# Attention scores of the window and sparse branches as full-array products, probabilities scaled on GpSimd

## The chip, the cores and the metric

The kernel runs on one core of a Trainium2 chip. TensorE (PE) does matrix products and transposes, VectorE (DVE), ScalarE (ACT) and GpSimd (POOL) do the rest, and DMA queues move data; the queue called SP here only issues DMAs. The metric is the device time of one execution in microseconds (us), the median of the runs.

## The reference, cut to what matters

A stack of layers on 512 tokens of width 1024 with 256 context tokens. Two layers of a first block hold, beside a convolution branch, a neighbourhood attention (NA) and a window attention (WA) with 8 heads of 64; later come a recurrent layer, a feed-forward layer, a sparse attention layer (NSA) with 16 heads and a second feed-forward layer. All values are float32. The parts that the change touches:

```python
# WA: block n of 128 queries sees up to 3 blocks of keys and 256 context keys
s_w = einsum('bqkgd,bskd->bkgqs', q_n, k_n) * scale
s_w = where(valid, s_w, -inf)
s_c = einsum('bqkgd,bnkd->bkgqn', q_n, k_ctx) * scale
m = maximum(max(concat([s_w, s_c]), axis=-1), sink)
e = exp(s - m)
p = e / (sum(e) + exp(sink - m))
# NSA: three branches (compressed, selected, window), each gated
s = einsum('bgrqd,bgkd->bgrqk', qc, kw)
s = s - slope * dist
p = masked_softmax(s, mask)
o = gc[0] * o_cmp + gc[1] * o_sel + gc[2] * o_win
```

## The kernel before, in words

**Number format.** Every float32 operand of a product is split into a rounded part (hi) and a rest (lo), `k.split` (L199 for the part on ACT, L200 for the rest on DVE). A product is then three: hi by hi, hi by lo, lo by hi. The large weights are loaded by SP, cast on ACT (L126, `wh`) and subtracted on DVE (L127, `wl`); their products stand at L140 to L142 (moving operand of 512 columns) and L151 to L153 (256 columns). These are called GEMM products here.

**Attention in units.** NA and WA are worked in units of one block of 128 queries (`attend`, L653). The score products of a unit (`att_qk`, `scores`, L484 to L490) write PSUM; `att_sm` makes probabilities; `att_tr` transposes them on PE (L582, L585) and copies them back; `pv` multiplies with V. In WA a pair of heads has one query block with both heads at its two ends (bands of 256 keys) and, for the two middle blocks, one unit for each head (bands of 384 keys): 16 one-head and 8 two-head units in a layer. In the first layer 8 further units come, of context queries, with 256 context keys alone. A unit is closed (transposed and multiplied) when more than three (WA) stand open.

**Half-array score products.** A head has 64 channels, and two heads lie on the two halves of the 128 partitions. The score products of before use 64 rows of the array each (form 64*128 in the trace): for one head three products, for two heads six, three in either half.

**Softmax of WA.** For each head: a maximum over the context scores (L543), a maximum with the sink (L545), an add of the mask with a running maximum over the band (L548), a negation (L551), the exponential on ACT (L553, or L556 and L557), the exponential of the sink (L561), sum and reciprocal, and the scaling of the probabilities on DVE (L570).

**NSA.** The loop L1530 to L1550 goes over 8 values of f (two heads each). In each f there are eight score units, two branches by four query blocks in the order 1, 3, 2, 0 with 256, 512, 384 and 256 columns, and one compressed unit. That makes 64 units: 32 of 256 columns, 16 of 384 and 16 of 512. L1459 has the scores, L1488 the mask and the maximum, L1490 the exponential, L1492 the scaling on DVE, L1524 the transposes, L1527 their copies. A unit is closed two units after its scores. `queries` (L1430) makes the queries of the next f as fill: 24 GEMM products, then `qf` (L1434) on DVE and the split into `nQ`.

**What sets the order.** A generator of attention steps is woven with a generator of GEMM steps: each attention step returns a cost, and GEMM steps are put behind it until the cost, times a ratio, is paid (`weave`, L55; in NSA the sum `due`, ratio 0.32). The framework's scheduler then sets the order on each engine from dependences and priorities, and puts in the waits.

Of the kernel before, what the change touches and what calls it, by code (L numbers as in the profile page):

```python
# [19 lines left out]
P = 128  # L20
# [16 lines left out]
NA_N, NW_N = (0, 0, 0, 0), (0, 0, 0, 0)  # L37
# [178 lines left out]
def first_block(k):  # L216
# [74 lines left out]
    for l in range(2):  # L291
# [120 lines left out]
        with tc.tile_pool(reuse_waits="tile", name=f"att{l}", bufs=2) as ap:  # L412
# [57 lines left out]

            def to_T_nat(raw, dst, g):
# [11 lines left out]

            def scores(heads, dst, Q, qi, K_, ki, q0, k0, kn):  # L484

                for a, b in ((0, 0), (0, 1), (1, 0)):
                    for i in heads:
                        sl = slice(64 * i, 64 * i + 64)
                        nc.tensor.matmul(dst[i], Q[sl, a, qi, q0:q0 + P], K_[sl, b, ki, k0:k0 + kn],  # L489
                                         start=a + b == 0, stop=a == 1)  # L490

            def att_qk(un):
# [35 lines left out]
                scores(heads, sc_, Q, qi, K_, ki, qb * P, 512, 256)  # L528
                if nb:
                    scores(heads, sb, Q, qi, K_, ki, qb * P, un["band"][0] * P, nb)  # L530
                return len(heads) * 3 * (256 + nb) / 2400

            nrm_ = [0]

            def att_sm(un):
# [3 lines left out]
                for i in un["heads"]:  # L539
# [3 lines left out]
                    V.tensor_reduce(m[:, 0:1], sc_, axis=AX.X, op=ALU.max)  # L543
                    if sink is not None:
                        V.tensor_max(m[:, 0:1], m[:, 0:1], sink)  # L545
                    mx = m[:, 0:1]
                    if nb:
                        V.tensor_tensor_reduce(out=sb, in0=sb, in1=un["bias"][i], scale=1.0, scalar=m[:, 0:1],  # L548
                                               op0=ALU.add, op1=ALU.max, accum_out=m[:, 1:2])
                        mx = m[:, 1:2]  # L550
                    V.tensor_scalar(m[:, 2:3], mx, -1.0, None, op0=ALU.mult)  # L551
                    if one:
                        AC.activation(pr, un["S"][i][:, :nb + 256], AF.Exp, bias=m[:, 2:3], accum_out=m[:, 3:4])  # L553
                        tot = m[:, 3:4]
                    else:
                        AC.activation(pr[:, nb:nb + 256], sc_, AF.Exp, bias=m[:, 2:3], accum_out=m[:, 3:4])  # L556
                        AC.activation(pr[:, :nb], sb, AF.Exp, bias=m[:, 2:3], accum_out=m[:, 4:5])  # L557
                        V.tensor_add(m[:, 5:6], m[:, 3:4], m[:, 4:5])
                        tot = m[:, 5:6]
                    if sink is not None:  # L560
                        AC.activation(m[:, 6:7], sink, AF.Exp, bias=m[:, 2:3])  # L561
# [4 lines left out]
                    nrm_[0] += 1  # L566
                    if (NA_N, NW_N)[not un["grp"]["na"]][nrm_[0] % 4]:
# [1146 lines left out]
```

## Time and profile before

| quantity | value |
|---|---|
| median of 3 runs | 2898.27 us (2898.22 to 2898.31) |
| profiled execution | 2899.95 us |
| its span, first to last instruction | 2898.1 us |
| mean granted TensorE clock | 0.993 of full speed |
| busy share of the span: PE, DVE, ACT, POOL | 98%, 67%, 38%, 0% |

The profile is of one execution. A row of the timeline gives the start, the duration, the engine, the line and operation, the output and inputs and their shape, and in brackets how long the engine was idle before and what released it. A row of several like instructions (x3) has the start of the first and the time until the last one's end. Ends of matrix products are modelled, so the time that a product holds PE is read from one start to the next, not from its duration. The stages of the attention branches are, in us from the span's start: NA of the first layer 117 to 254, WA 328 to 480, NA of the second layer 1000 to 1115, WA 1172 to 1275, NSA 2235 to 2440.

### The profile page before, as it was taken

What the parts mean: (1) busy time and instruction counts of PE and PEld (TensorE: products, weight loads), DVE (VectorE), ACT (ScalarE), POOL (GpSimd) and SP (SyncE); (2) the same over time, 40 slices, a digit from 0 to 9 for tenths busy, and PEclk for the clock granted to TensorE, in tenths of its full rate; (3) what the DMA queues carried; (4) which work ended last, traced back from release to release, by engine and by line L of the source; (5) the groups of instructions that cost most, each with busy time, mean ns of one, the idle gap of its engine ahead of it and who ended that gap; (6) DMA issues with size and microseconds to landing.
All of it is one profiled execution on the core that took longest, in us unless ns stands there. A gap on an engine that the chain in (4) does not pass through costs nothing.

```text
span 2898.1 us, 41445 instructions
## 1 busy us (share of the span) xinstructions
PE 2839.2 (98%) x15812; PEld 2313.7 (80%) x15812; DVE 1941.7 (67%) x4673; ACT 1114.6 (38%) x2218; POOL 0.7 (0%) x6
## 2 busy tenths in 40 slices
PE   6999999999999999999999999999999999999998
PEld 3987877888887888778888878888888666888886
DVE  5767788994544667999757866636543777663663
ACT  3444454122222444542334743223333766322221
POOL 0000000000000000000000000000000000000000
PEclk8999999999999999999999999999999999999999
DMA  6211111432125221112233233232243001223322
GB/s 219 69 62 46 36 33 42 146 131 73 66 73 161 84 74 62 44 59 91 99 106 105 95 96 100 89 107 95 88 134 103 23 16 52 95 93 97 102 89 78
DMA packets 79542, 248.68 MB, mean 86 GB/s; under 512 B 8944, under 2 KB 16496, under 8 KB 79344
## 3 DMA queue, kind: packets, MB, share of 16 engines
q1 hardware_dynamic: 75888, 238.69, 25.6%
q10 hardware_dynamic: 3456, 7.34, 0.8%
q8 instruction: 125, 2.05, 0.3%
q14 instruction: 73, 0.60, 0.1%
HBM read 239.71 MB, written 4.19 MB: 84 GB/s over the span
## 4 chain that ended last, share of the span: by engine, by line
PE 88%; DVE 5%; ACT 2%; issue 1%; DMA 0%; DVEq 0%; ACTq 0%
PE g L140 22%; PE g L142 22%; PE g L141 22%; PE g L151 3%; PE g L153 2%; PE g L152 2%; PE s L489 2%; PE g L1508 1%; PE o L609 1%; PE t L585 1%; PE t L582 1%; PE s L1459 1%; PE s L516 1%; PE t L1524 1%; PE o L630 1%
## 5 line engine op out<-in xcount | busy, mean ns | idle before, releaser
L126 ACT CAST wh<-wr 128x1024 fp32r<-128x1024 f32 (+2 forms) x392 | 392.3, 1002 | 839.0 <-PE g L141 581.8
L140 PE MATMUL g<-Hh,wh 128*128 128x512 f32 x1736 | 691.1, 398 | 0.5 <-DVE Yb L1255 0.4
L141 PE MATMUL g<-Hl,wh 128*128 128x512 f32 x1736 | 682.2, 393 | 0.0
L142 PE MATMUL g<-Hh,wl 128*128 128x512 f32 x1736 | 681.3, 392 | 0.0
L127 DVE TENSOR_TENSOR wl<-wr,wh 128x1024 fp32r<-128x1024 f32 (+2 forms) x392 | 455.2, 1162 | 304.8 <-ACT wh L126 303.9
L140 PEld LDWEIGHTS g<-Hh,wh 128*128 128x128 f32 x1736 | 326.6, 188 | 75.7 <-issue 5.9
L142 PEld LDWEIGHTS g<-Hh,wl 128*128 128x128 f32 x1736 | 326.1, 188 | 71.9 <-issue 2.3
L141 PEld LDWEIGHTS g<-Hl,wh 128*128 128x128 f32 x1736 | 326.6, 188 | 63.7 <-issue 1.0
L151 PE MATMUL g<-wh,Hh 128*128 128x256 f32 x640 | 187.6, 293 | 1.6 <-ACT Hh L359 1.3
L915 DVE SCALAR_TENSOR_TENSOR cv<-apad,cv 128x499 f32<-128x499 f32 (+23 forms) x305 | 187.1, 668 | 0.6
L153 PE MATMUL g<-wh,Hl 128*128 128x256 f32 x640 | 183.0, 287 | 0.0
L152 PE MATMUL g<-wl,Hh 128*128 128x256 f32 x640 | 182.9, 286 | 0.0
L141 PE MATMUL g<-fl,wh 128*128 128x512 f32 x384 | 149.6, 390 | 0.0
L142 PE MATMUL g<-fh,wl 128*128 128x512 f32 x384 | 149.6, 390 | 0.0
L140 PE MATMUL g<-fh,wh 128*128 128x512 f32 x384 | 149.6, 390 | 0.0
L151 PEld LDWEIGHTS g<-wh,Hh 128*128 128x128 f32 x640 | 123.1, 192 | 9.5 <-issue 5.9
L153 PEld LDWEIGHTS g<-wh,Hl 128*128 128x128 f32 x640 | 122.4, 192 | 4.5 <-issue 2.9
L152 PEld LDWEIGHTS g<-wl,Hh 128*128 128x128 f32 x640 | 123.0, 192 | 1.7 <-issue 1.2
L1276 DVE TENSOR_TENSOR fxp<-g,nb 128x512 f32<-128x512 f32 x48 | 33.2, 692 | 127.4 <-PE g L142 127.4
L553 ACT ACTIVATE pr<-s,m 128x512 f32<-128x512 f32 (+1 forms) x128 | 80.6, 633 | 76.8 <-DVE m L551 65.9
L1168 DVE TENSOR_TENSOR Xs<-Xs,g 128x512 f32<-128x512 f32 x48 | 33.0, 688 | 113.0 <-PE g L142 112.9
L140 PE MATMUL g<-Ch,wh 128*128 128x256 f32 x352 | 101.2, 287 | 0.0
(403 smaller groups left out, 5249.7 us busy)
## 6 DMA issues: line engine op xcount, KB each, us to landing
wr<-in_ffn_w_in_dram SPq DMA_DIRECT2D x96, 512.0 KB, 3.5
wr<-in_w_in_t_dram SPq DMA_DIRECT2D x88, 512.0 KB, 3.5
wada<-in_w_ada_dram SPq DMA_DIRECT2D x48, 512.0 KB, 4.6
wr<-in_ffn_w_out_dram SPq DMA_DIRECT2D x64, 384.0 KB, 3.1
wr<-in_w_in_n_dram SPq DMA_DIRECT2D x32, 512.0 KB, 3.8
wr<-in_lru_w_in_dram SPq DMA_DIRECT2D x20, 512.0 KB, 3.5
wr<-in_w_o_dram SPq DMA_DIRECT2D x16, 512.0 KB, 3.6
bt<-in_nab_dram SPq DMA_DIRECT2D x48, 128.0 KB, 2.4
```

Of the source, the lines that this page charges most:

```text
L126: nc.scalar.copy(h[:, :n], r[:, :n])
L127: nc.vector.tensor_sub(lo[:, :n], r[:, :n], h[:, :n].bitcast(F32))
L140: mm(o, a, hi(k), start=k == 0, stop=False)
L141: mm(o, a, lo(k), start=False, stop=False)
L142: mm(o, b, hi(k), start=False, stop=k == KT - 1)
L151: mm(o, h, w[k][0], start=k == 0, stop=False)
L152: mm(o, h, w[k][1], start=False, stop=False)
L153: mm(o, lo(k)[:, t0:t0 + P], w[k][0], start=False, stop=k == KT - 1)
L489: nc.tensor.matmul(dst[i], Q[sl, a, qi, q0:q0 + P], K_[sl, b, ki, k0:k0 + kn], start=a + b == 0, stop=a == 1)
L553: AC.activation(pr, un["S"][i][:, :nb + 256], AF.Exp, bias=m[:, 2:3], accum_out=m[:, 3:4])
L915: V.scalar_tensor_tensor(d, src, wc, d, op0=ALU.mult, op1=ALU.add)
L1276: V.tensor_mul(xp[:, 2:514], o, rb)
```

## The change

**Scores.** The two WA and NSA score functions now use all 128 rows. A query tile of one head holds its hi part on one half of the partitions and its lo part on the other half; the keys stand doubled on both halves. One product with the keys' hi part gives hi by hi plus lo by hi, a second with the keys' lo part gives hi by lo plus lo by lo: two products for each head where there were three. The part that lies on the wrong half is first made in a helper tile (`tmp`, `qx`) and brought over by DMA: in WA two DMAs for each transposed group, issued from POOL (`swap`), in NSA two of 64x512 (128 KB each) for each f, issued from SP. Casts and subtractions go over half the partitions, two of each instead of one. Bands of 256 and context are scored together in 512 columns.

**Softmax of WA.** One instruction over band and context adds the mask (zeros for the context), negates, and takes the running minimum from the negated sink; the maximum over the context, the one with the sink and the negation go. With a band of 384 keys there are two such instructions.

**Scaling.** All probabilities (160 instructions in NA and WA, 128 in NSA) are scaled on POOL instead of DVE.

**Costs for the order.** The score steps return two thirds of the cost they returned, so less GEMM work is put between.

```diff
             def to_T2(raw, dst, g, gain, tmp):
...
+                for lo, h, l_ in ((0, d4[0:64, :, 0, c], x[0:64]), (64, x[64:128], d4[64:128, :, 1, c])):
+                    sl = slice(lo, lo + 64)
+                    AC.activation(h, tv[sl], AF.Identity, scale=gain[sl])
+                    V.scalar_tensor_tensor(l_, tv[sl], gain[sl], h.bitcast(F32), op0=ALU.mult, op1=ALU.subtract)
+                swap(d4, x, c)
+            def swap(d4, x, c):
+                nc.gpsimd.dma_start(out=d4[64:128, :, 0, c].bitcast(F32), in_=x[0:64].bitcast(F32))
+                nc.gpsimd.dma_start(out=d4[0:64, :, 1, c].bitcast(F32), in_=x[64:128].bitcast(F32))
+            def to_T2_nat(raw, dst, g, tmp):
...
+                if g == 1:
+                    swap(dst.rearrange("p (a i) n -> p a i n", i=2), tmp, slice(0, S))
-            def scores(heads, dst, Q, qi, K_, ki, q0, k0, kn):
+            def scores(na, heads, dst, Q, qi, K_, ki, q0, k0, kn):
+                if not na:
+                    for i in heads:
+                        for b in range(2):
+                            kk = K_[:, b, ki, k0[0]:k0[0] + kn]
...
+                            nc.tensor.matmul(dst[i], Q[:, 2 * qi + i, q0:q0 + P], kk, start=b == 0, stop=b == 1)
+                    return
-                return len(heads) * 3 * (256 + nb) / 2400
+                return len(heads) * (3 if na else 2) * (256 + nb) / 2400
...
+                        both = one and nb
+                        for x, bias, to in (((un["S"][i], wmz(un["bias"][i], z), m[:, 1:2]),) if both else
+                                            ((sc_, z, m[:, 0:1]),) + (((sb, un["bias"][i], m[:, 1:2]),) if nb else ())):
...
+                            V.tensor_tensor_reduce(out=x, in0=x, in1=bias, scale=-1.0, scalar=mx,
+                                                   op0=ALU.add, op1=ALU.min, accum_out=to)
+                            mx = to
...
-                        V.tensor_scalar(pr, pr, rc, None, op0=ALU.mult)
+                    G.tensor_scalar(pr, pr, rc, None, op0=ALU.mult)
...
-                k.split(Q[:, 0], Q[:, 1], qf)
+                k.split(Q[0:64, 0], qx[0:64], qf[0:64])
+                k.split(qx[64:128], Q[64:128, 1], qf[64:128])
+                nc.sync.dma_start(out=Q[64:128, 0].bitcast(F32), in_=qx[0:64].bitcast(F32))
+                nc.sync.dma_start(out=Q[0:64, 1].bitcast(F32), in_=qx[64:128].bitcast(F32))
...
-                for x, y in ((0, 0), (0, 1), (1, 0)):
-                    for i in range(2):
-                        nc.tensor.matmul(S_[i][:, :nn], Q[sls[i], x, qb * P:(qb + 1) * P], KS[b][sls[i], y, g, :nn],
-                                         start=x + y == 0, stop=x == 1)
-                return 6 * nn / 2400
+                for i in range(2):
+                    for y in range(2):
+                        nc.tensor.matmul(S_[i][:, :nn], Q[:, i, qb * P:(qb + 1) * P], KS[b][:, y, g, :nn],
+                                         start=y == 0, stop=y == 1)
+                return 4 * nn / 2400
...
-                    V.tensor_scalar(pr[:, :nk], pr[:, :nk], m[:, 2:3], GT[:, qb, h:h + 1], op0=ALU.mult, op1=ALU.mult)
+                    G.tensor_scalar(pr[:, :nk], pr[:, :nk], m[:, 2:3], GT[:, qb, h:h + 1], op0=ALU.mult, op1=ALU.mult)
```

The order on PE in the first WA stage of the first layer, before; the names s are score tiles in PSUM, g the GEMM output, kw and qw the WA keys and queries:

```order
L152 MATMUL g_3855<-wl_3758,Hh_99 128x256
L489 MATMUL s_3931<-kw_3024,qw_3449 128x256 x3
L153 MATMUL g_3855<-wh_3757,Hl_100 128x256
L151 MATMUL g_3855<-wh_3751,Hh_99 128x256
L152 MATMUL g_3855<-wl_3752,Hh_99 128x256
L153 MATMUL g_3855<-wh_3751,Hl_100 128x256
L151 MATMUL g_3855<-wh_3751,Hh_99 128x256
L152 MATMUL g_3855<-wl_3752,Hh_99 128x256
L489 MATMUL s_3932<-kw_3024,qw_3449 128x384 x3
L153 MATMUL g_3855<-wh_3751,Hl_100 128x256
```

The same place after (the score line is now L531, the GEMM lines L150 to L152):

```order
L152 MATMUL g_3876<-wh_3767,Hl_100 128x256
L531 MATMUL s_3882<-kw_3026,qw_3451 128x512 x2
L531 MATMUL s_3911<-kw_3026,qw_3451 128x256 x2
L531 MATMUL s_3912<-kw_3026,qw_3451 128x384 x2
L150 MATMUL g_3876<-wh_3773,Hh_99 128x256
L151 MATMUL g_3876<-wl_3774,Hh_99 128x256
L531 MATMUL s_3932<-kw_3026,qw_3451 128x256 x2
L152 MATMUL g_3876<-wh_3773,Hl_100 128x256
```

Three score products of 256 or 384 columns have become two, and a two-head unit two pairs of 512 columns.

The order on PE in NSA between one f and the next, before: transposes of the old f (L1524), then the scores of the new f (L1459, nQ is its query tile), with the compressed scores (L1451) between:

```order
L1524 MATMUL t_21478<-ident,pr_21407 128x128 x4
L1524 MATMUL t_21484<-ident,pr_21407 128x128 x4
L1451 MATMUL s_21500<-KC,qf_21201 128x62 x4
L1524 MATMUL t_21516<-ident,pr_21435 128x128 x3
L1524 MATMUL t_21521<-ident,pr_21435 128x128 x3
L1459 MATMUL s_21526<-KS_20040,nQ_21492 128x256
L1459 MATMUL s_21527<-KS_20040,nQ_21492 128x256
L1459 MATMUL s_21526<-KS_20040,nQ_21492 128x256
L1459 MATMUL s_21527<-KS_20040,nQ_21492 128x256
L1459 MATMUL s_21561<-KS_20040,nQ_21492 128x512
L1459 MATMUL s_21562<-KS_20040,nQ_21492 128x512
L1459 MATMUL s_21561<-KS_20040,nQ_21492 128x512
```

The same place after (L139 to L141 GEMM, L1602 transposes, L1586 products with V, L1579 transposes of the compressed unit); g_21210 is the output from which the new f's queries are made, g_21514 that of the f after it:

```order
L141 MATMUL g_21210<-Hh_19239,wl_21207 128x512
L1602 MATMUL t_21457<-ident,pr_21388 128x128 x3
L1602 MATMUL t_21462<-ident,pr_21388 128x128 x3
L1602 MATMUL t_21502<-ident,pr_21418 128x128
L1602 MATMUL t_21505<-ident,pr_21418 128x128
L139 MATMUL g_21514<-Hh_19239,wh_21510 128x512
L140 MATMUL g_21514<-Hl_19240,wh_21510 128x512
L1586 MATMUL g_21539<-PT_21287,VS_19714 64x512
L1586 MATMUL g_21539<-PT_21288,VS_19714 64x512
L1586 MATMUL g_21539<-PT_21287,VS_19714 64x384
L141 MATMUL g_21514<-Hh_19239,wl_21511 128x512
L1579 MATMUL t_21535<-ident,pc_21446 124x128
```

The last product of the query GEMM now stands ahead of the last transposes, and GEMM products of the f after it and products with V stand where the new scores stood.

The order on ACT at the same place, before:

```order
L1490 ACTIVATE pr_21467,m_21468<-s_21459,m_21468 128x128
L199 CAST nQ_21492<-qf_21490 128x512
L1490 ACTIVATE pr_21467,m_21473<-s_21460,m_21473 128x128
L126 CAST wh_21553<-wr_21551 128x1024
L1527 COPY PT_21446<-t_21516 128x3x128
L1527 COPY PT_21447<-t_21521 128x3x128
```

and after, where L198 is the cast of the split (nQ, and qx in the helper tile), L125 the cast of the weights, L1519 the scaled bias and L1605 the copies of transposed probabilities:

```order
L198 CAST nQ_21472<-qf_21470 64x512
L125 CAST wh_21510<-wr_21508 128x1024
L198 CAST qx_21473<-qf_21470 64x512
L1519 ACTIVATE M_21480<-nb_19238 128x512 x2
L1605 COPY PT_21399<-t_21502 128x128
L1605 COPY PT_21400<-t_21505 128x128
```

The one cast of the queries is two, with the cast of the next weights between them.

## Rows read from the trace of the kernel before

**Rows 1.** page, busy time of each engine, share of the span and instructions

```profile
PE 2839.2 (98%) x15812; PEld 2313.7 (80%) x15812; DVE 1941.7 (67%) x4673; ACT 1114.6 (38%) x2218; POOL 0.7 (0%) x6
```

**Rows 2.** page, chain that ended last: share of the span by engine

```profile
PE 88%; DVE 5%; ACT 2%; issue 1%; DMA 0%; DVEq 0%; ACTq 0%
```

**Rows 3.** windows, WA stage of both layers and sparse stage: us, busy (count) by engine, clock

```profile
328.00:480.00 152.00, 149.81 (x939) 113.92 (x939) 128.98 (x527) 77.79 (x242) 0.00 (x0) 1.00 0.10 31
...
1172.00:1275.00 103.00, 102.76 (x576) 71.77 (x575) 91.72 (x359) 56.98 (x172) 0.00 (x0) 1.00 0.11 37
...
2235.00:2440.00 205.00, 200.12 (x1315) 130.63 (x1313) 156.77 (x600) 146.86 (x446) 0.00 (x0) 0.99 0.08 24
```

**Rows 4.** timeline of PE, first layer, one-head unit: start us, us, instruction

```profile
334.99 0.28 PE L151 MATMUL g<-wh,Hh 128*128 128x256 f32 x1
335.11 0.28 PE L152 MATMUL g<-wl,Hh 128*128 128x256 f32 x1
335.32 0.61 PE L489 MATMUL s<-kw,qw 64*128 64x256 f32 x3
335.86 0.39 PE L153 MATMUL g<-wh,Hl 128*128 128x256 f32 x1
...
336.77 0.78 PE L489 MATMUL s<-kw,qw 64*128 64x384 f32 x3
337.48 0.39 PE L153 MATMUL g<-wh,Hl 128*128 128x256 f32 x1
```

**Rows 5.** lines by form, PE, first WA stage: score products, busy and mean ns

```profile
L489 PE MATMUL s<-kw,qw 64*128 64x256 f32 x192 | 27.5, 307 | 0.2
...
L489 PE MATMUL s<-kw,qw 64*128 64x384 f32 x48 | 11.9, 353 | 0.0
```

**Rows 6.** timeline of PE, sparse stage, groups of 256 and 512 columns

```profile
2277.21 0.40 PE L142 MATMUL g<-Hh,wl 128*128 128x512 f32 x1
2277.53 0.62 PE L1459 MATMUL s<-KS,nQ 64*128 64x256 f32 x6
2278.09 0.88 PE L1524 MATMUL t<-ident,pr 128*128 128x128 f32 x6
2278.89 0.96 PE L1459 MATMUL s<-KS,nQ 64*128 64x512 f32 x6
2279.78 0.33 PE L1524 MATMUL t<-ident,pr 128*128 128x128 f32 x1
```

**Rows 7.** lines by form, DVE, first WA stage and sparse stage: count, busy us, mean ns

```profile
L570 DVE TENSOR_SCALAR pr<-pr,rc 128x512 f32<-128x512 f32 x16 | 7.7, 482 | 0.2
...
L1492 DVE TENSOR_SCALAR pr<-pr,m,GT 128x512 f32<-128x512 f32 x32 | 17.4, 544 | 0.4
```

**Rows 8.** lines by form, POOL, whole program

```profile
masks.py:199 POOL TENSOR_SCALAR_AFFINE_SELECT ident<-ident 128x128 f32<-128x128 f32 x1 | 0.3, 292 | 0.1
```

**Rows 9.** DMA issues: line, queue, count, KB each, median us to landing

```profile
bt<-in_nab_dram SPq DMA_DIRECT2D x48, 128.0 KB, 2.4
...
cD<-ct SPq DMA_DIRECT2D x4, 256.0 KB, 3.9
```

**Rows 10.** timeline of all engines, start of the sparse stage

```profile
2237.62 0.39 PE L142 MATMUL g<-Hh,wl 128*128 128x512 f32 x1
...
2238.78 0.62 ACT L199 CAST nQ<-qf 128x512 fp32r<-128x512 f32 x1 [5.35 <-DVE qf L1434]
...
2239.30 1.05 ACT L126 CAST wh<-wr 128x1024 fp32r<-128x1024 f32 x1
...
2239.43 0.69 DVE L200 TENSOR_TENSOR nQ<-qf,nQ 128x512 fp32r<-128x512 f32 x1 [0.68 <-ACT nQ L199]
...
2239.45 1.34 PE L1459 MATMUL s<-KS,nQ 64*128 64x256 f32 x8 [1.43 <-ACT nQ L199]
```

**Rows 11.** windows, just behind that start

```profile
2240.00:2244.00 4.00, 4.00 (x13) 2.21 (x13) 3.28 (x9) 3.58 (x8) 0.00 (x0) 0.64 0.21 56
```

**Rows 12.** waits in the sparse stage: us in total, times, longest us

```profile
PEld s L1459 <- ACT nQ L199: 5.2, 7, 1.9
```

More of the change, by code (lines that the diff above doesn't have):

```diff
@@ L527, in att_qk @@
                 un["sc"], un["sb"] = sc_, sb
-                scores(heads, sc_, Q, qi, K_, ki, qb * P, 512, 256)
-                if nb:
-                    scores(heads, sb, Q, qi, K_, ki, qb * P, un["band"][0] * P, nb)
-                return len(heads) * 3 * (256 + nb) / 2400
-            nrm_ = [0]
+                na = un["grp"]["na"]
+                if nb == 256:
+                    two = lambda v: v.rearrange("p (s n) -> p s n", s=2)
+                    scores(na, heads, {i: two(S_[i]) for i in heads}, Q, qi, K_, ki, qb * P, (un["band"][0] * P, S), 256)
+                else:
+                    scores(na, heads, sc_, Q, qi, K_, ki, qb * P, (S,), 256)
+                    if nb:
+                        scores(na, heads, sb, Q, qi, K_, ki, qb * P, (un["band"][0] * P,), nb)
+                return len(heads) * (3 if na else 2) * (256 + nb) / 2400
+            nsk = lc.tile([P, 8], F32, tag="nsk", name=k.nm("nsk"), bufs=2)
+            V.tensor_scalar(nsk, co[:, C_SINK:C_SINK + 8], -1.0, None, op0=ALU.mult)
+            zero = []
             def att_sm(un):
@@ L551, in att_sm @@
-                    V.tensor_scalar(m[:, 2:3], mx, -1.0, None, op0=ALU.mult)
+                        sg, mx = -1.0, nsk[:, un["head"][i]:un["head"][i] + 1]
+                        z = un["zero"]
+                        both = one and nb
+                        for x, bias, to in (((un["S"][i], wmz(un["bias"][i], z), m[:, 1:2]),) if both else
+                                            ((sc_, z, m[:, 0:1]),) + (((sb, un["bias"][i], m[:, 1:2]),) if nb else ())):
+                            if both:
+                                x = x.rearrange("p (s n) -> p s n", s=2)
+                            V.tensor_tensor_reduce(out=x, in0=x, in1=bias, scale=-1.0, scalar=mx,
+                                                   op0=ALU.add, op1=ALU.min, accum_out=to)
+                            mx = to
+                    else:
+                        V.tensor_reduce(m[:, 0:1], sc_, axis=AX.X, op=ALU.max)
+                        mx = m[:, 0:1]
+                        if nb:
+                            V.tensor_tensor_reduce(out=sb, in0=sb, in1=un["bias"][i], scale=1.0, scalar=mx,
+                                                   op0=ALU.add, op1=ALU.max, accum_out=m[:, 1:2])
+                            mx = m[:, 1:2]
+                        V.tensor_scalar(m[:, 2:3], mx, -1.0, None, op0=ALU.mult)
+                        mx = m[:, 2:3]
@@ L565, in att_sm, with wmz @@
                     V.reciprocal(rc, tot)
[L566 to L570 removed]
+                    G.tensor_scalar(pr, pr, rc, None, op0=ALU.mult)
+            def wmz(bias, z):
+                return bass.AP(tensor=bias.tensor, offset=bias.offset,
+                               ap=[list(bias.ap[0]), [z.offset - bias.offset, 2], [1, 256]])
             def att_tr(un):
@@ L664, in attend @@
                                           "qi": pr, "K": Kt, "ki": kis[pr],
-                                          "sink": {i: sinkf(4 * u + 2 * pr + i) for i in heads}})
+                                          "sink": {i: sinkf(4 * u + 2 * pr + i) for i in heads},
+                                          "head": {i: 4 * u + 2 * pr + i for i in heads}, "zero": natural and zero[0]})
                 def close(un):
```

61 lines of the change are left out of this document (40 added, 21 removed).

## The prediction

> **What bounds the kernel now.** I read the busy times first: TensorE (PE) is busy for 98% of the span, VectorE (DVE) for 67%, GpSimd (POOL) not at all [rows 1]. The chain that ended last says the same in another way: 88% of it is PE [rows 2]. So a saving counts only where it takes time off PE, and a wait costs as soon as PE has nothing else in its queue. Then the windows of the three stages that the change reaches: PE is busy for 149.81 of 152 us and 102.76 of 103 us in the two WA stages and 200.12 of 205 in the sparse one; DVE has 23, 11 and 48 us to spare there [rows 3]. Moving work off DVE buys nothing by itself. What is to be gained is the score products' time on PE; what can be lost is PE's full queue. The timeline of PE gives the products' real price, from start to start.
>
> **WA scores.** GEMM products of 256 columns start 0.12 us apart; when a half-array product follows, 0.21, so entering a half-array group costs 0.09. A one-head unit holds PE for 0.54 us with its three products of 256 columns and for 0.71 with its three of 384 [rows 4]. With two entries that is 1.43 us. After the change it is two products of 0.12 and two of some 0.175 (between 0.12 and the 0.23 of 512 columns, below), 0.59 us, so 0.84 less. The 48 products of 384 columns in the first stage [rows 5] are 16 such units, 32 in both layers: 27 us. Where context and band stand without GEMM between, an entry less is saved; I take 25. The other 24 units (16 with two heads, 8 of context queries; part of the 192 products of 256 columns [rows 5]) run their heads side by side, as the sparse groups below, and gain about 0.15 each, 4 us. WA: -29. If the entry is not due to the half array it stays, which leaves about 21; if leaving a group also costs something that I have not counted, it is some 6 more.
>
> **Sparse scores.** A GEMM product of 512 columns takes 0.32 with an entry behind it, so 0.23 without. A group of six products of 256 columns holds PE for 0.56 us, one of 512 for 0.89 [rows 6]; with the entry 0.65 and 0.98. Four full products are 0.48 and 0.92; for 384, between, about 0.81 and 0.70. So the 64 units save 32 x 0.17 + 16 x 0.11 + 16 x 0.06 = 8 us; groups broken into two or three parts by the scheduler pay more entries, and I take -10 (ends -4, the entry stays, and -16).
>
> The gain per unit is small where both halves were in use, since the pairs already ran side by side.
>
> **The swap in the sparse stage.** Here the change adds a wait. Today the first score needs only the cast: from the last GEMM product at 2237.62 to the score at 2239.45 it is 1.83 us, with PE idle for 1.43 [rows 10]. Afterwards a score needs lo and hi on opposite halves: after the cast (0.62) the subtraction (0.69) [rows 10] and a DMA within the chip. None like it is in the trace: a load of the same 128 KB lands after 2.4 us, a copy of 256 KB inside the chip after 3.9 [rows 9]. I take 2.4, the nearer size; with 3.9 as the upper end and nothing but the subtraction as the lower. At the start there is little to fill it: +3.1 (0.7 to 4.6).
>
> At the seven later borders between one f and the next PE waits today 5.2 us in all for the cast, 0.74 each [rows 12]. By the new order the last query product stands before some eight transposes (0.9 us), then two GEMM products of the f after it, three products with V and one GEMM product (1.3 us together at 0.23 or less), then the scores; on ACT the cast of those GEMM weights (1.05) [rows 10] stands behind the first query cast and before the second. From the last product the cast starts after 1.16 us [rows 10], ends at 1.78, the subtraction at 2.47, the DMA at 4.9. Of these 4.9 us PE fills 2.2: idle 2.7, 2.0 more than now, 14 us at seven borders. Ends: 3 (the DMA lands in 0.8 us) and 28 (3.9 us, and the second cast behind the weights' cast). Queued behind the swap on SP are weight loads that are wanted one f later; I cost them at nothing, since the dearer DMA lands in 3.9 us [rows 9] and an f lasts 25 (205 over 8); without that cover they would lengthen the same border.
>
> **The clock.** Behind the 1.43 us of idle the granted clock is 0.64 in the 4 us from 2240 [rows 11], against 0.99 over the stage [rows 3]: 1.4 us lost. Seven idles of 2.7 us could each do that, up to 10 us; I take half, +5 (0 to 10).
>
> **Scaling on POOL.** The trace has one POOL operation of some size: 128x128 in 0.292 us [rows 8], so 512 columns cost at most four times that, 1.17; at least what DVE takes, 0.48 in WA and 0.54 in the sparse stage [rows 7]. I take 0.8, between, so 0.3 more for each instruction. It counts only as latency, since 128 sparse and 160 other ones fill POOL to less than half of a stage. The sparse loop keeps two units open: two scales of mean 320 columns, 0.38 us more, over two units 0.19, times 64 is 12 us if nothing hides it. PE's 200 of 205 busy us [rows 3] say that most is hidden now, and the freed DVE shortens the same chain: +2 (0 to 25). In WA three units are open; 0.3 to 0.7 us for each instruction, two in a two-head unit, is at most 10 us over 48 units; GEMM fill covers about half, +5 (0 to 10). The WA swap stands in POOL's queue among the scales and behind GEMM work; I cost it inside these 5. In the neighbourhood stages only the scale moves: 0 (-3 to +8).
>
> On that price the Trainium skill, page "GPSIMD Engine Reference", section 4.1 Engine selection, says that elementwise work with one input runs at about line rate on GpSimd; no row here shows it. By it the scale would cost what it does on DVE, and the sum would be 7 us lower.
>
> **Shorter softmax, less GEMM put between.** The maxima and the negation leave DVE, which has room in WA [rows 3]: 0. Smaller step costs move GEMM products later, none away: 0, and their price is in the borders.
>
> **Sum.** -29 + 5 (WA) - 10 + 3 + 14 + 5 + 2 (sparse) = -10. The profiled execution took 2899.95 us, 2898.1 of it span and 1.85 around; 2899.95 - 10 = 2890. The median of the runs is 1.7 lower than the profiled one, so I forecast 2888.
>
> **Rivals.**
> - *The swap is hidden.* The DMA lands in about 1 us, or PE's queue holds enough: without the 14 and the 5 it is 2869, and without the 5 of WA 2864. For it speaks that transposes and products with V, needed anyway, can stand in front; against it, that the order shows only 2.2 us of them.
> - *POOL paces the units.* At 1.17 us for 512 columns the scales cost 25 and 10 in place of 2 and 5: 2916, slower. In a straight line between, it turns the sum to slower from about 0.96 us. For it speaks the one POOL row, four times as dear per column as DVE's scale; against it, that this row may be mostly fixed cost. The Trainium skill, page "SBUF — State Buffer", section SBUF: two separate sides, adds a reason: a port pair that DVE and GpSimd share is locked for a whole instruction, so a DVE operation with two SBUF inputs would hold up a scale. No row of before shows it, with POOL idle.
> - *The longer border.* The DMA takes 3.9 us and the second cast waits: 28 in place of 14, 2902.
> - *Entries stay.* The 0.09 us belongs to the change of work, not to the half array: WA -21, sparse -4, 2902. Against it speaks that GEMM products of different tiles follow without it [rows 4].
>
> **How the numbers follow.** Forecast 0.45, with its own range 2879 to 2897; swap hidden 0.20; POOL paces 0.18; longer border 0.11; entries stay 0.06. The range runs from the first rival's 2864 to 2911, a little short of the second's 2916. What a measurement can tell from no change is 0.2%, 5.8 us: below 2892.5 it is faster, above 2904.1 slower. The forecast's case gives 0.33 faster and 0.12 no change, the hidden swap 0.20 faster, POOL 0.03 faster, 0.04 no change and 0.11 slower, the last two together 0.02, 0.08 and 0.07. That makes 0.58, 0.24 and 0.18.
>
> **What would show it.** In the profile after: score products of form 128*128 starting 0.12 to 0.23 us apart, with no entry of 0.09; the WA stages together shorter by about 24 us; eight waits of the sparse scores for a DMA with PE idle 2 to 3 us each, and the clock below 1 behind them; POOL scales of 512 columns near 0.8 us. The forecast is wrong if PE's idle at the borders stays under 1 us (then faster), or if the copies of transposed probabilities or the transposes wait for POOL all through the sparse stage (then slower).

## The result, and the profile after

The changed kernel takes 2943.08 us (median of 4 runs, 2940.37 to 2947.11); the kernel before, measured again beside it, 2898.24. The ratio is 1.016, 95% interval 1.0147 to 1.0172: slower by 45 us, where 10 us less were forecast and 2911 was the range's upper end.

**POOL.** The page of the changed kernel first, busy times and chain, which answer to [rows 1, 2]:

```profile
PE 2827.5 (96%) x15476; PEld 2318.6 (79%) x15476; DVE 1876.7 (64%) x4277; ACT 1133.5 (39%) x2252; POOL 336.4 (11%) x308
...
PE 81%; DVE 8%; ACT 3%; POOL 2%; issue 2%; DMA 1%; DVEq 0%; ACTq 0%; POOLq 0%
```

PE is busy for 12 us less and the span is 44 us longer: PE waits. For whom it waits is said by the view of POOL's lines by form (count, busy us, mean ns, idle before), which answers to [rows 8] and, for the scale on DVE, [rows 7]:

```profile
L633 POOL TENSOR_SCALAR pr<-pr,rc 128x512 f32<-128x512 f32 x96 | 153.1, 1606 | 840.9 <-DVE rc L632 811.1 <-DVE m L625 9.3 <-DVE rs_i L159 7.9
L633 POOL TENSOR_SCALAR pr<-pr,rc 128x640 f32<-128x640 f32 x32 | 63.5, 1991 | 45.3 <-DVE rc L632 18.3 <-PE g L140 6.9 <-DVE m L625 6.5
L633 POOL TENSOR_SCALAR pr<-pr,rc 128x256 f32<-128x256 f32 x32 | 32.3, 1018 | 20.6 <-DVE rc L632 12.5 <-ACT pr L620 3.2 <-ACT PT L665 2.5
L1570 POOL TENSOR_SCALAR pr<-pr,m,GT 128x512 f32<-128x512 f32 x32 | 24.4, 773 | 14.9 <-DVE m L1569 14.8
```

The two scale lines do not cost the same. That of the sparse stage (L1570) multiplies by two factors and takes 773 ns for 512 columns, as taken in the sum (0.8 us). That of NA and WA (L633) multiplies by one and takes 1606, twice as long, above the 1.17 us that had been the upper end.

What it does is seen in the timeline of an NA stage (start us, us, instruction, idle before and releaser), around the scale of one unit:

```profile
264.28 3.11 POOL L633 TENSOR_SCALAR pr<-pr,rc 128x512 f32<-128x512 f32 x2 [3.68 <-DVE rc L632]
...
265.90 0.44 PE L650 MATMUL t<-ident,pr 128*128 128x128 f32 x2 [0.60 <-POOL pr L633]
...
267.44 0.44 PE L650 MATMUL t<-ident,pr 128*128 128x128 f32 x2 [0.89 <-POOL pr L633]
```

Two heads are scaled one after the other in 3.11 us, and each one's transposes (L650) start when its scale ends. Only one NA unit stands open ahead of another, so little other work covers it. The list of waits has the sum over the program (us, times, longest us), weight load and product apart:

```profile
PEld t L650 <- POOL pr L633: 46.2, 54, 2.2
...
PE t L650 <- POOL pr L633: 30.1, 39, 2.0
```

In NA these waits are only half of the loss. The windows of the first NA stage, of the changed kernel, of e2 (the same kernel with the scale in its two-factor form) and of e3 (the kernel before with the scaling as changed), have the granted clock as the third number from the end:

```profile
114.00:287.00 173.00, 160.08 (x1085) 128.01 (x1084) 95.49 (x361) 71.00 (x183) 66.75 (x48) 0.95 0.16 49
```

```profile
114.00:267.00 153.00, 150.55 (x1086) 122.15 (x1084) 94.83 (x360) 69.82 (x183) 31.02 (x48) 1.00 0.18 56
```

```profile
115.10:280.90 165.80, 152.50 (x1079) 121.53 (x1079) 95.17 (x358) 70.78 (x183) 65.74 (x48) 1.00 0.16 51
```

Against e2 the changed kernel's stage is 20 us longer: PE is idle for 10.5 us more (12.9 against 2.4), and it is busy for 9.5 us more with as many products, at a mean granted clock of 0.95 instead of 1.00. In e3, with the clock at 1.00, the same scale costs the stage 13.6 us. POOL is busy for 67 of the 173 us, so it is its latency and not its capacity that counts.

**The score products** came out as worked out where GEMM products stand around them. In the timeline of PE, which answers to [rows 4], two score products of 256 columns hold PE for 0.24 us (357.66 to 357.90), with 0.12 from the GEMM product before them, no entry (behind a transpose the same two take 0.32, 370.69 to 371.01):

```profile
357.54 0.28 PE L151 MATMUL g<-wl,Hh 128*128 128x256 f32 x1
357.66 0.40 PE L531 MATMUL s<-kw,qw 128*128 128x256 f32 x2
357.90 0.28 PE L152 MATMUL g<-wh,Hl 128*128 128x256 f32 x1
```

**The stages.** The windows of the two WA stages and the sparse stage, at their later places ([rows 3]; us, busy by engine and count, granted clock):

```profile
353.00:492.00 139.00, 128.83 (x784) 101.15 (x784) 120.47 (x414) 86.53 (x266) 76.94 (x54) 0.99 0.13 37
1210.00:1318.00 108.00, 97.71 (x506) 68.21 (x507) 88.64 (x285) 60.40 (x187) 59.66 (x34) 0.98 0.14 42
2276.00:2489.00 213.00, 202.53 (x1209) 142.58 (x1208) 128.15 (x486) 153.81 (x458) 79.18 (x128) 0.96 0.12 35
```

PE has 10 us of idle in each where it had 2, 0 and 5. At a border of the sparse stage PE now waits for the cast of the next weights, which stands between the two query casts, and the mean granted clock of the 20 us around it is 0.91. A timeline row, the wait over the stage (2.4 us of it at the stage's start, 6.2 at six borders), the window and the new DMA (count, KB, us to landing), which answer to [rows 9 to 12]:

```profile
2322.09 0.50 PE L139 MATMUL g<-Hh,wh 128*128 128x512 f32 x1 [1.07 <-ACT wh L125]
```

```profile
PE g L139 <- ACT wh L125: 8.6, 7, 2.4
```

```profile
2320.00:2340.00 20.00, 18.50 (x107) 12.22 (x107) 9.73 (x36) 11.63 (x34) 4.82 (x8) 0.91 0.15 41
```

```profile
nQ<-qx SPq DMA_DIRECT2D x16, 128.0 KB, 2.2
```

The swap's DMA lands after 2.2 us (2.4 were taken), and PE's waits of the stage have no score that waits for it.

**Where the time went, all kernels.** The same landmarks (first score of a stage, last product with V, last copy) were read from each kernel's profiled execution. The table has the change of each stretch against the kernel before, in us; the stretch of the second WA runs on through the layers behind it to the start of the sparse layer, and the last column is start and end of the program. The ratio of the medians stands with its interval; times are medians. The stretches are of one execution each: kernels with the same first block agree there to about 1.5 us a column, but e13 and e14, with the same sparse code, differ by 3.1 in the sparse one, and the columns of e2 add up to -4.7 where the medians say 0. Differences of 3 us in the sparse column are at the edge of what they can tell.

| kernel | time, us | ratio | NA 1 | WA 1 | NA 2, with the work between | WA 2, to the sparse layer | sparse | rest |
|---|---|---|---|---|---|---|---|---|
| changed | 2943.1 | 1.0160 (1.0147 to 1.0172) | +19.9 | -12.3 | +21.5 | +8.1 | +7.8 | -1.0 |
| e1_scale_dve | 2920.2 | 1.0076 (1.0061 to 1.0091) | 0.0 | -14.6 | +10.7 | -1.9 | +25.9 | +0.5 |
| e2_two_factor | 2898.4 | 1.0001 (0.9992 to 1.0011) | -0.2 | -16.7 | +9.4 | -1.4 | +4.7 | -0.5 |
| e3_pool_only | 2944.1 | 1.0158 (1.0143 to 1.0173) | +13.6 | +5.2 | +13.3 | +10.2 | -2.5 | +0.9 |
| e4_sparse_scores | 2925.7 | 1.0088 (1.0072 to 1.0105) | -0.1 | -0.1 | +0.1 | -0.3 | +30.5 | -3.3 |
| e6_wa_only_two_factor | 2889.3 | 0.9971 (0.9961 to 0.9982) | -0.1 | -15.8 | +9.8 | -0.8 | -1.7 | -0.3 |
| e7_old_costs | 2895.9 | 0.9993 (0.9984 to 1.0003) | -0.2 | -5.6 | +1.1 | -0.5 | +0.5 | +2.2 |
| e8_no_swap | 2876.3 | 0.9930 (0.9915 to 0.9945) | -0.1 | -16.8 | +9.7 | -1.5 | -14.0 | -0.8 |
| e9_pool_two_factor | 2904.8 | 1.0029 (1.0019 to 1.0039) | -0.2 | +1.7 | +0.9 | +3.3 | -1.2 | +1.0 |
| e10_early_queries | 2906.3 | 1.0034 (1.0021 to 1.0047) | +0.2 | -16.6 | +9.3 | -1.7 | +14.3 | -0.5 |
| e11_dve_no_swap | 2905.4 | 1.0028 (1.0017 to 1.0039) | 0.0 | -0.1 | +0.3 | -0.2 | +6.4 | -2.4 |
| e12_no_swap_at_all | 2871.2 | 0.9910 (0.9895 to 0.9925) | +0.3 | -21.9 | +10.2 | -5.5 | -12.5 | -0.4 |
| e13_shift | 2894.0 | 0.9988 (0.9978 to 0.9997) | +0.2 | -16.7 | +10.6 | -0.9 | +1.7 | +0.4 |
| e14_shift_both | 2900.4 | 1.0009 (1.0000 to 1.0019) | -0.1 | -14.9 | +10.5 | +2.7 | -1.4 | 0.0 |
| e15_lead_one | 2889.8 | 0.9975 (0.9965 to 0.9984) | -0.1 | -15.8 | +9.8 | -1.7 | -2.0 | -0.5 |
| e16_lead_two | 2887.2 | 0.9966 (0.9953 to 0.9979) | +0.3 | -16.8 | +9.9 | -2.2 | -4.5 | -0.7 |
| e17_lead_dma | 2888.8 | 0.9972 (0.9962 to 0.9983) | -0.1 | -16.7 | +10.0 | -1.5 | -3.1 | -0.3 |

The +10 behind the first WA stage in most rows is GEMM work that the smaller step costs no longer weave into that stage; it is read together with the column before it.

### The profile page after: what moved, and what is told of

It is laid out like the page before. It is cut to its first block, busy times and chain, and to the rows that moved or that the text cites. A ratio compares the mean times of both kernels' runs of the same rounds, so it can differ in the third digit from the quotient of the medians.

```text
span 2942.1 us, 41222 instructions
## 1 busy us (share of the span) xinstructions
PE 2827.5 (96%) x15476; PEld 2318.6 (79%) x15476; DVE 1876.7 (64%) x4277; ACT 1133.5 (39%) x2252; POOL 336.4 (11%) x308
## 4 chain that ended last, share of the span: by engine, by line
PE 81%; DVE 8%; ACT 3%; POOL 2%; issue 2%; DMA 1%; DVEq 0%; ACTq 0%; POOLq 0%
PE g L139 21%; PE g L140 21%; PE g L141 20%; PE g L150 2%; PE g L152 2%; POOL pr L633 2%; PE g L151 2%; PE g L1586 2%; PE s L1537 1%; DVE wl L126 1%; PE o L677 1%; PE t L1602 1%; PE t L650 1%; PE t L653 1%; PE s L531 1%
## 5 line engine op out<-in xcount | busy, mean ns | idle before, releaser
L125 ACT CAST wh<-wr 128x1024 fp32r<-128x1024 f32 (+2 forms) x392 | 392.3, 1001 | 846.1 <-PE g L140 589.2
L139 PE MATMUL g<-Hh,wh 128*128 128x512 f32 x1736 | 688.3, 396 | 9.1 <-ACT wh L125 8.6
L141 PE MATMUL g<-Hh,wl 128*128 128x512 f32 x1736 | 681.3, 392 | 0.5 <-DVE wl L126 0.5
L139 PEld LDWEIGHTS g<-Hh,wh 128*128 128x128 f32 x1736 | 326.2, 188 | 83.6 <-ACT wh L125 10.9
L141 PEld LDWEIGHTS g<-Hh,wl 128*128 128x128 f32 x1736 | 326.3, 188 | 74.2 <-issue 5.6
L633 POOL TENSOR_SCALAR pr<-pr,rc 128x512 f32<-128x512 f32 (+2 forms) x160 | 248.5, 1565 | 906.8 <-DVE rc L632 842.0
L1570 POOL TENSOR_SCALAR pr<-pr,m,GT 128x256 f32<-128x256 f32 (+3 forms) x128 | 79.2, 631 | 1090.8 <-DVE m L1569 1090.0
L150 PE MATMUL g<-wh,Hh 128*128 128x256 f32 x640 | 187.8, 294 | 1.6 <-ACT Hh L358 1.3
L989 DVE SCALAR_TENSOR_TENSOR cv<-apad,cv 128x503 f32<-128x503 f32 (+24 forms) x305 | 186.3, 664 | 0.5
L152 PE MATMUL g<-wh,Hl 128*128 128x256 f32 x640 | 184.3, 289 | 0.0
L139 PE MATMUL g<-fh,wh 128*128 128x512 f32 x384 | 149.4, 389 | 0.0
L141 PE MATMUL g<-fh,wl 128*128 128x512 f32 x384 | 149.4, 389 | 0.0
L150 PEld LDWEIGHTS g<-wh,Hh 128*128 128x128 f32 x640 | 124.4, 194 | 8.4 <-issue 5.3
L152 PEld LDWEIGHTS g<-wh,Hl 128*128 128x128 f32 x640 | 123.8, 194 | 5.0 <-issue 3.4
```

Source lines behind the costliest of these rows:

```text
L125: nc.scalar.copy(h[:, :n], r[:, :n])
L139: mm(o, a, hi(k), start=k == 0, stop=False)
L141: mm(o, b, hi(k), start=False, stop=k == KT - 1)
L150: mm(o, h, w[k][0], start=k == 0, stop=False)
L152: mm(o, lo(k)[:, t0:t0 + P], w[k][0], start=False, stop=k == KT - 1)
L633: G.tensor_scalar(pr, pr, rc, None, op0=ALU.mult)
```

## The experiments

Four questions: what the scaling costs, what the scores cost, what the swap costs, and whether the swap can be had cheaper.

**e1_scale_dve** has both scale lines back on DVE:

```diff
-                    G.tensor_scalar(pr, pr, rc, None, op0=ALU.mult)
+                    V.tensor_scalar(pr, pr, rc, None, op0=ALU.mult)
```

(and L1570 in the same way).

> The changed kernel with all 288 probability scalings back on DVE; everything else as changed. Theory P (the scaling on POOL, 1.6 us for 512 columns in NA and WA, is a latency that PE waits for): the 31 us that the two NA stages lost come back, and some 10 of WA, so about 2898 - 5 = 2893 us (2885 to 2903); NA of the first layer again lasts 152 us from first score to last product with V instead of 172. Rival S (the loss is in the borders: the swaps by DMA, the shorter fill): NA does gain its own loss back only in part and the time stays above 2920 us.

It took 2920.2 us, 17 above the upper end of theory P. The first NA stage gave its 19.9 us back to the last tenth, as theory P says, but the sparse stage went from +7.8 to +25.9, which neither theory had: there the scale on POOL had been a help.

**e2_two_factor** changes the form of the one scale line and nothing else:

```diff
-                    G.tensor_scalar(pr, pr, rc, None, op0=ALU.mult)
+                    G.tensor_scalar(pr, pr, rc, 1.0, op0=ALU.mult, op1=ALU.mult)
```

> The changed kernel, with the NA and WA scaling on POOL written with two factors (the reciprocal and the constant 1.0) as the sparse one is, instead of one factor. Theory F (the one-factor form itself is slow on POOL: 1606 ns for 512 columns against 773 in the sparse stage): the row falls to about 0.77 us for 512 columns and the time to 2943 - 20 = about 2922 us (2910 to 2930). Rival C (it is the stage, DVE working beside it in NA and WA, that makes POOL slow): the row stays near 1.6 us and the time at 2943.

It took 2898.4 us, 45 less than the changed kernel. POOL's lines of this run (count, busy us, mean ns):

```profile
L633 POOL TENSOR_SCALAR pr<-pr,rc 128x512 f32<-128x512 f32 x96 | 68.3, 720 | 881.0 <-DMA wr<-in_w_in_n_dram 531.3 <-DVE rc L632 307.9 <-DVE rs_i L159 14.2
L633 POOL TENSOR_SCALAR pr<-pr,rc 128x640 f32<-128x640 f32 x32 | 28.0, 877 | 75.9 <-DVE rc L632 29.1 <-PE g L140 9.1 <-ACT PT L665 9.0
...
L633 POOL TENSOR_SCALAR pr<-pr,rc 128x256 f32<-128x256 f32 x32 | 18.5, 586 | 36.1 <-DVE rc L632 17.0 <-ACT pr L620 4.1 <-ACT PT L665 4.1
```

720 ns against 1606, in the same places, with the same DVE work beside it: the form is slow and not the stage. Why this form takes twice as long is not shown. Theory F is right in its cause; its price of 20 us was less than half of what came.

**e3_pool_only** is the kernel before with only the two scale lines on POOL, as changed.

> The kernel before, with only the 288 scalings moved to POOL; scores and softmax as before. Theory P: the NA stages lose the same 31 us, WA some 10, the sparse stage 0 to 10: 2935 to 2948 us. Rival S: at most 5 us slower than before, 2898 to 2903.

2944.1 us, as the changed kernel to 1 us: the scaling alone, with the one-factor form in NA and WA, costs as much as the whole change loses, and the sparse stage does not lose by it (-2.5). That the rest of the change sums to nothing is what e2 says. By stages the two kernels differ (first NA stage +13.6 against +19.9, by the clock).

**e9_pool_two_factor** is the same with two factors.

> The kernel before with all scalings on POOL, two factors everywhere, nothing else. Theory: 0.72 us on POOL in place of 0.48 on DVE is hidden, and the freed DVE shortens the chain of each unit: 2888 to 2896 us. Rival: DVE was never waited for long, so 2896 to 2900; if latency counts as in the one-factor run, above 2903.

2904.8 us, slower than before by 0.29% (0.19 to 0.39): even at 0.72 us the scale costs some latency where DVE's 0.48 was hidden, 5 us over the two WA columns, and DVE's freed time gives at most 1 us back, in the sparse stage. The theory missed, and the last clause of the rival (above 2903) holds.

**e4_sparse_scores** is the kernel before with the sparse scores, their swap and their cost as changed (the last hunks of the diff), scaling on DVE.

> The kernel before, with only the sparse scores as full-array products, their swap by DMA and their smaller cost; scaling on DVE. Theory B (the wait for the swap and the weights' cast at the eight borders outweighs the shorter products): about +10 us, 2905 to 2912. Rival P2 (in the changed kernel the sparse stage lost because of POOL's latency): the shorter products show, about -8 us, 2888 to 2893.

2925.7 us, +30.5 in the sparse stage, three times what theory B had. The windows of ten us ahead of a border, behind it and after (granted clock is the third number from the end) show why, and PE's first instruction at the border:

```profile
2310.00:2320.00 10.00, 8.78 (x54) 6.81 (x52) 8.88 (x35) 9.07 (x32) 0.00 (x0) 1.00 0.00 0
2320.00:2330.00 10.00, 8.92 (x29) 3.55 (x30) 4.61 (x12) 3.80 (x8) 0.00 (x0) 0.66 0.28 80
2330.00:2340.00 10.00, 9.81 (x69) 7.63 (x68) 6.70 (x27) 5.44 (x18) 0.00 (x0) 1.00 0.00 2
```

```profile
2321.08 0.66 PE L1505 MATMUL t<-ident,pc 128*124 128x128 f32 x2 [1.57 <-DVE pc L1482]
```

After 1.57 us of idle the granted clock of the window is 0.66, most of it at 1.2 GHz: by this mean 3.4 us lost behind 1.6 of idle. Six of the seven borders show such a window (0.66 to 0.71).

**e8_no_swap** is the two-factor kernel with the old split in place of the two splits and the two DMAs.

```diff
...
-                k.split(Q[0:64, 0], qx[0:64], qf[0:64])
-                k.split(qx[64:128], Q[64:128, 1], qf[64:128])
-                nc.sync.dma_start(out=Q[64:128, 0].bitcast(F32), in_=qx[0:64].bitcast(F32))
-                nc.sync.dma_start(out=Q[0:64, 1].bitcast(F32), in_=qx[64:128].bitcast(F32))
+                k.split(Q[:, 0], Q[:, 1], qf)
```

> The two-factor kernel without the swap by DMA in the sparse stage: hi and lo of a query tile are left on their own halves, so the sparse scores are not those of the reference; products, sizes and scaling stay. Theory B (the wait for subtraction, DMA and casts at the borders costs what the shorter products gain): the sparse stage goes from +7 to about -8 against before, 2882 to 2887 us. Rival: the borders wait for the weights' cast whatever the swap does, 2893 to 2898.

2876.3 us, 6 below theory B's range; sparse -14.0 where the two-factor kernel has +4.7. The placing of lo beside hi (its DMAs and the doubled casts and subtractions) costs 19 us there, 22 by the medians, and the full-array products are worth 13 (14.0 less e9's 1.2; 13.0 by the medians of e6 and this run). Every window of 20 us of that stage has a clock of 1.00.

**e11_dve_no_swap** is e4 without the swap, in the same way.

> The kernel before with the sparse scores as full-array products, scaling on DVE, and no swap (hi and lo stay on their own halves, so these scores are not the reference's). Theory K (of the 28 us that the sparse scores with the swap lost here, the swap's idle and the half clock behind it are the cause): about 2898 - 10 = 2888 us (2884 to 2892), granted clock of the stage 0.99 again. Rival: it is the scaling on DVE with the new order of units that loses it, above 2910.

2905.4 us, between theory K's range and its rival's, +6.4 in the sparse stage: theory K accounts for 24 of e4's 30.5 (20 by the medians), not for the rest. With scaling on DVE the first score of a border waits for the query cast still (6.5 us over the stage, 6 times), and the clock of the stage is 0.96. That DVE's queue lengthens the chain through `qf` is likely; it was not tried by itself.

**e12_no_swap_at_all** leaves the swap out in WA too.

> The two-factor kernel with no swap in the WA branches either (nor in the sparse one): hi and lo of the queries stay on their own halves, so the output is not the reference's. Theory S (the first block kept only 12 of the 26 us that its products save because PE waits for the swap ahead of WA): the first block gains 6 to 12 us more, 2864 to 2871 us. Rival L (the units' own latency, with less GEMM between them, keeps it): 2873 to 2878, as without the sparse swap alone.

2871.2 us, at theory S's upper end. The first block gains 8.2 us against e8 (sum of the four columns: -16.9 against -8.7); the medians are 5.1 apart, so the swap ahead of WA costs 5 to 8 us.

**e7_old_costs** has the old step costs (`3 * (256 + nb)` and `6 * nn`) in the two-factor kernel.

> The two-factor kernel with the old step costs (three products for each head in WA, 6 x columns in the sparse stage), so as much GEMM work is woven between as before. Theory W (part of the shorter products is lost because too little GEMM stands between units and ahead of the borders): PE's idle in the WA and sparse stages falls and the time by 5 to 12 us, to 2886 to 2893. Rival: the idle is the swap's own and stays, 2895 to 2901.

2895.9 us: 2.5 us better than e2, at the edge of what can be told, and in the rival's range. The sum hides two things: the sparse stage gains 4.2, and the first block gives up 3.7 (-5.2 in the four columns against -8.9).

**e6_wa_only_two_factor** takes the sparse scores back to those of before and keeps the rest of e2.

> WA scores and softmax as changed, all scaling on POOL with two factors, the sparse scores as before. Theory: the parts add up. The first block keeps the 12 us that the two-factor run gained there, the sparse stage keeps its old products and loses the borders: 2898 - 12 - 2 = about 2884 us (2880 to 2888). Rival: the two-factor run's sparse stage was no loss, then this stays near 2896.

2889.3 us, faster than the kernel before by 0.29% (0.18 to 0.39). The parts add up within 5 us (1.3 above the theory's range), and the sparse stage is again the -2 of e3.

**e10_early_queries** weaves the next query GEMM at a ratio of 0.6 instead of 0.32 in e2.

> The two-factor kernel with one number changed: the ratio at which the sparse stage weaves in the next query GEMM, 0.6 in place of 0.32, so that it ends some units before the border. Theory B (the swap costs 21 us because it starts only at the border): most of it is hidden, the sparse stage goes from +7 to about -8 against before, 2882 to 2888 us. Rival: fill that is spent early is missing behind the transposes later, and the stage gains under 5 us: 2893 to 2898.

2906.3 us, worse than e2 by 8 and above the rival's range too: theory B in this form falls. PE's waits over the sparse stage, behind its start, name the new one:

```profile
PE s L1537 <- ACT pr L1568: 13.4, 21, 1.6
PE g L141 <- DVE wl L126: 1.7, 3, 0.6
PE g L139 <- ACT wh L125: 0.8, 1, 0.8
```

The fill is spent by the fourth unit, and the later scores wait for the exponential to free their PSUM.

**e13_shift** does the sparse placing without DMA: the subtraction reads one half of the partitions and writes the other (the two splits, the two DMAs and the helper tile go).

```diff
...
+                AC.copy(Q[0:64, 0], qf[0:64])
+                AC.copy(Q[64:128, 1], qf[64:128])
+                V.tensor_sub(Q[64:128, 0], qf[0:64], Q[0:64, 0].bitcast(F32))
+                V.tensor_sub(Q[0:64, 1], qf[64:128], Q[64:128, 1].bitcast(F32))
```

> The two-factor kernel with the sparse swap done without DMA: the subtraction on DVE reads one half of the partitions and writes its result onto the other half, so hi and lo of a head lie together; the DMAs and the helper tile are gone. Theory D (the 21 us at the borders are the DMA's latency and the clock behind it): as without the swap, 2875 to 2880 us. Rival (any chain of cast, subtraction and placing is too long there, or the subtraction across halves is slow): 2888 to 2898.

2894.0 us, sparse +1.7, only 3 us better than with the DMA (4 by the medians; e14, with the same sparse code, is 6 better). Theory D falls: the DMA's own time is the smaller part of the price. The waits of the stage still have the first score waiting, now for the subtraction, 2.2 us at the start and 5 at six borders:

```profile
PEld s L1536 <- DVE nQ L1513: 8.8, 7, 2.6
...
PE s L1536 <- DVE nQ L1513: 7.2, 7, 2.2
```

**e14_shift_both** does so in the WA branches too.

> The same in the WA branches too, so that no swap by DMA is left. Theory D: both gains together, near the 2871 us of the kernel without swaps, 2867 to 2875. Rival: WA's start waits for the halves all the same, 2876 to 2882.

2900.4 us, no better than before (1.0009, 1.0000 to 1.0019), and far above the ranges of theory and rival: the sparse stage gains 3, the WA stages lose 5 against e13. Why WA is worse with the shift than with its DMA stays open.

**e15_lead_one, e16_lead_two, e17_lead_dma** move the last query product ahead of the border by a smaller step than e10, ratios 0.36 and 0.4 in e13 and 0.4 in e2.

> The kernel with the subtraction's placing, weaving ratio of the sparse stage 0.36 in place of 0.32: by the sum of costs the last query product comes about one unit ahead of the border. Theory L (the border's price is the chain behind a product that comes too late): the sparse stage gains 5 to 10 us, 2884 to 2889. Rival: fill that is missing behind the last units costs as much, 2892 to 2896.

> The same with ratio 0.4, about two units ahead. Theory L: the chain is hidden, 2880 to 2886, unless the missing fill shows already. Rival: as at 0.6, units without fill wait for the exponential: above 2894.

> The two-factor kernel with its swap by DMA and ratio 0.4. Theory L: with two units of lead the DMA's 2.2 us are hidden as well, within 3 us of the run with the subtraction's placing at 0.4. Rival: the DMA is still late by one unit, 5 us or more slower than that.

2889.8, 2887.2 and 2888.8 us; sparse -2.0, -4.5 and -3.1 where ratio 0.32 gave +1.7 and +4.7. The gain has theory L's direction in all three and its rivals are out; e15 and e16 stay 1 us above its ranges, so a little less is hidden than it says. With two units of lead the DMA is as good as the shift. PE's waits in the sparse stage of e16, behind its start (the first line is the compressed unit's scores):

```profile
PE s L1528 <- ACT pr L1567: 2.3, 5, 0.5
...
PE g L139 <- ACT wh L125: 1.7, 5, 0.3
...
PE s L1536 <- DVE nQ L1513: 0.9, 1, 0.9
```

Only one border still waits for its query tile. e16 beats both kernels: 0.9966 of the kernel before (0.9953 to 0.9979), 56 us less than the changed one. Of the 14 us that e8 showed, 4.5 are had.

## Why the prediction was wrong

- **Scaling on POOL: the step that failed.** 0.8 us was taken for 512 columns, with 1.17 as upper end; two lines of different form were given one price. The two-factor line took 0.77 for 512 columns, so the 0.8 was right for 128 of 288 instructions. The one-factor line took 1.61, above the bound, because the bound was made from the only POOL row of before [rows 8], an operation of another kind (nor is it four times as dear per column as DVE's scale, as the rival has it: 0.292 over 128 against 0.482 over 512 is 2.4 times). The form is worth 45 us: changed against e2.
- **Its reach: NA at 0 (-3 to +8).** The changed kernel loses 20 us there in the first layer and, against e2, 12 in the second. Half of the first layer's 20 is PE idle behind POOL, half a lower granted clock (0.95), a cost that the prediction had for the sparse borders alone. NA keeps one unit open; WA keeps three and lost 14 (changed against e2: 4 and 10 in the two columns). The sentence "in the neighbourhood stages only the scale moves: 0" skipped the question that was asked for the sparse loop, how many units cover the latency. The rival "POOL paces the units" named the right mechanism and had 0.18; its 2916 was built on the same two errors, and put the loss in the sparse stage and WA, where changed against e2 has 32 of 49 us in the two NA columns. Its turning point of 0.96 us is a slip too: on the straight line the sum of -10 is used up at 0.93.
- **WA scores: -29, measured -26** in PE's busy time over the first block. These are the sums of the windows from the first NA score to the end of the block, of the kernel before and of e2:

```profile
sum 1515.20, PE 1501.78 PEld 1244.73 DVE 1124.89 ACT 581.92 POOL 0.00; mean PE 187.72 PEld 155.59 DVE 140.61 ACT 72.74 POOL 0.00
```

```profile
sum 1505.60, PE 1476.12 PEld 1231.87 DVE 1087.80 ACT 592.73 POOL 122.79; mean PE 184.51 PEld 153.98 DVE 135.97 ACT 74.09 POOL 15.35
```

  PE works 25.7 us less and the stretch is 9.6 shorter: 16 us came back as idle, where 5 were taken for the scaling. The scaling, in its two-factor form, does cost about these 5 (e9), and the swap ahead of WA 5 to 8 more (e12 against e8), which the prediction had "inside these 5".
- **Sparse scores: -10, measured -13** (e8, less e9). Right within its ends.
- **The swap at the borders: 3 + 14, and 5 for the clock, 22 in all; measured 19** by the stretches, 22 by the medians (e2 against e8). The size was right, the parts were not, so the agreement is partly luck. The sign that was named, scores that wait for a DMA with PE idle for 2 to 3 us, did not come: PE waits about 1 us at six borders, for the weights' cast. These are the windows from the end of the work before the stage to its last copy, of e2 and of e8:

```profile
2208.70:2440.10 231.40, 218.01 (x1336) 157.46 (x1334) 134.80 (x502) 159.37 (x467) 79.10 (x128) 0.98 0.13 37
```

```profile
2208.70:2421.40 212.70, 204.54 (x1336) 153.94 (x1335) 126.23 (x494) 150.70 (x461) 78.50 (x128) 1.00 0.09 31
```

  Of the 18.7 us between them only 5.2 are idle of PE, where 17 were forecast; for 13.5 PE counts as busy longer with the same 1336 products. The clock, 0.98 against 1.00, makes some 5 of these (an estimate: 0.02 of 231); the rest stays open. The DMA, 2.2 us, could be left out for a gain of 3 to 6 (e13, e14). More is had by its place: the last query product stands at the border, with the chain of `qf`, cast and subtraction behind it, and moving it two units ahead gives 6 to 8 (e13 to e16, e2 to e17).
- **Scaling in the sparse stage: +2 (0 to 25), measured a gain.** That the freed DVE "shortens the same chain" outweighs POOL's latency there: moving the scale from DVE to POOL gains 21 us with the new scores (e1 to e2) and 1 us with the old ones (e9).
- The Trainium skill, page "GPSIMD Engine Reference", section 4.1 Engine selection, says that elementwise work with one input runs at roughly line rate on GpSimd. Read as DVE's price, as the prediction did, it is not borne out by the trace: 720 ns with two factors and 1606 with one, against DVE's 482 [rows 7]. The Trainium skill, page "SBUF — State Buffer", section SBUF: two separate sides, has a port pair that DVE and GpSimd share and that one of them holds for a whole instruction. That lock does not explain the slow form: e2 had the same DVE work beside it.

Had the one-factor line run at 0.72 us, the kernel would have come out at 2898, inside the range and still no gain; the forecast of 2888 would have been 10 off. Behind that stand two errors of opposite sign: by e2's stretches the first block came out 15 us worse than the -24 of the sum (-9), and the sparse stage 9 better than its +14 (+5).

## What to carry to other kernels

Price an instruction on a new engine in the very form that will be issued, and give every stage its own answer to "how many units are open while this runs". Where a change lengthens a chain at a loop's border, first look at where the work that starts the chain stands in the order: moving that by two units was worth 6 to 8 us, taking the DMA out 3 to 6. A PE saving that leaves short idles behind can cost more than it gains: in e4 the shorter products ended in a loss of 30 us, with six stretches of ten us at a granted clock of 0.66 to 0.71.

## What the runs showed that was not expected

- POOL's multiplication of a 128x512 float32 tile by one factor for each partition takes 1606 ns, by that factor and a constant 720 (e2); the cost for each further column is (1991 - 1018) / 384 = 2.5 ns against (877 - 586) / 384 = 0.76.
- A DVE subtraction of 64x512 that writes the other half of the partitions takes 685 ns (e13), one that stays on its half 690 to 699 (e2), so two halves can be exchanged with no DMA.
- In e4 idles of about 1.6 us at a border were followed by ten us with a mean granted clock of 0.66, and in the changed kernel's first NA stage waits of up to 2.0 us for POOL went with a mean of 0.95 over 173 us.
